# Moving the streamed and loaded operands of a matmul to other distances in SBUF, stage by stage

## The chip, the cores and the metric

One core of a Trainium2 chip runs the whole program. The metric is the device time of one execution in microseconds (us). The kernel before takes 986.3 us, the median of three runs (985.2 to 988.33).

## The reference

256 tokens of width 1024 go through one attention and feed-forward layer and then through two recurrent layers, all in float32.

```python
def reference(x, ...):
    x = first_block(x, mem, positions, ...)
    return second_block(x, c_2, ...)

def _layer(x, mem, positions, ...):
    h = _rms_norm(x, g_pre_mix)
    proj = h @ w_in                                   # 1024 x 8864
    y_mla, y_dil, y_mem = ...                         # three attention branches
    merged = gates0 * (y_mla @ w_br_mla) + gates1 * (y_dil @ w_br_dil) + gates2 * (y_mem @ w_br_mem)
    x = x + _rms_norm(merged @ w_o, g_post_mix)
    h2 = _rms_norm(x, g_pre_ffn)
    return x + _rms_norm(_conv_ffn(h2, w_ffn_up, conv_w, conv_b, w_ffn_down), g_post_ffn)

def second_block(x, c, ...):
    for l in range(2):
        h = rms_norm(x, norm_g[l]) * (1 + scale) + shift
        rg_x, rg_z, ml_x, ml_o, ml_z = split(h @ w_in[l])      # five products of 1024 x 1024
        y_rg = rglru(conv(rg_x)) * silu(rg_z)
        y_ml = mlstm_branch(ml_x, ml_o) * silu(ml_z)
        x = x + gate * (concatenate([y_rg, y_ml]) @ w_out[l])
    return rms_norm(x, final_g)
```

## The kernel before, in words

Nearly all of TensorE's time goes to products of activations with weights, and each is made of three matmuls. `load` (line 246) brings a block of weights of 128x1024 float32 from memory into a `raw` tile, ScalarE rounds it into `hi` (line 254) and VectorE takes the rest into `lo` (line 257). The activations are kept as two tiles in the same way, `H` and `L`. `prod` (line 261) then adds hi x H, hi x L and lo x H into PSUM. A matmul of TensorE has two operands: `lhsT` is loaded into the array (a weight load, PEld in the profile), `rhs` is streamed through it (PE). The weight load of a matmul runs while the matmul before it streams.

There are two roles:

- In `proj` (line 269) the weights are loaded, 128 columns at a time, and the activations are streamed, 256 columns at a time. In the profile these are `mm<-H,hi`, `mm<-L,hi` and `mm<-H,lo`; 48 of them make one projection of 256 output columns, and the page puts 16 of each kind to it. This is the H role.
- In `proj_long` (line 286) the activations are loaded, 128 tokens at a time, and the weights are streamed, 256 columns at a time. These are `mm<-hi,s` and `mm<-lo,s`, the output products: `w_o`, `w_down`, `w_out0` and `w_out1`. This is the O role. The values of the dilated attention (`w_dv`) use the same function with `H` and `L` as the loaded operand (`mm<-hi,H`).

There are four stages that fill `H` and `L` anew and then use them: the attention mix (29 projections, 33 to 335 us), the feed-forward's `w_up` (22, 358 to 481 us), layer 0 (20, 558 to 723 us) and layer 1 (20, 772 to 935 us). Each ends in its output product: `w_o`, `w_down`, `w_out0`, `w_out1`.

Where the operands lie is set by the pools. The rings for `hi` and `lo` start at 224 bytes modulo 256, and every 128-column or 256-column piece of them too. `H` and `L` (line 351) start at 160 modulo 256. The large slots of `sp` hold the loaded operands of the output products (`gH`, `gL`, `aH`, `aL`, `yrH`, `yrL`, `ymH`, `ymL`) at 32 modulo 256, and with `stream=True` other operands at 160. So the distance, the streamed address minus the address that is being loaded for the next matmul, modulo 256, is 192 in both roles: 160 - 224 and 224 - 32. The exceptions are the dilated values at 224 - 160 = 64, and single pairs of 0, 64 and 128 where one kind of matmul follows another, as where `of_head` (line 967) puts two matmuls of `selR` between two projections.

The scheduler of the Tile layer orders the instructions.

Of the kernel before, what the change touches and what calls it, by code (L numbers as in the profile page):

```python
# [10 lines left out]
F32 = mybir.dt.float32  # L11
F32R = mybir.dt.float32r
# [6 lines left out]
P = 128  # L19
S = 256  # L20
D = 1024
KT = D // P
# [5 lines left out]
RAW, HI, LO = 4, 4, 4  # L28
FENCE = 4
STREAM = 32  # L30
HOLD = 3
MIX = """gc0 lr ms0 gc1 ln ms1 mt0 gc2 my0 ms2 mt1 lq0 my1 lq1 ms3 mt2 lq2 my2 lq3 mt3 lk my3 lv gc3
    ls0 bc0 bc1 ls1 bc2 bc3 lt0 dp0 ly0 ls2 lt1 x1 dp1 ly1 ls3 lt2 x1 dp2 ly2 ls4 lt3 x1 dp3 ly3 ls5 lt4 x1 dp4 ly4 ls6 lt5 x1 dp5 ly5 ls7 lt6 x1 dp7 ly6 lt7 x1 ga0 ly7 x1 dp6 x1
# [164 lines left out]
def block_kernel(ctx: ExitStack, tc: tile.TileContext, T: dict, out: bass.AP):  # L198
# [3 lines left out]
    cp = ctx.enter_context(tc.tile_pool(name="cp", bufs=1))  # L202
# [3 lines left out]
    fill = ctx.enter_context(tc.tile_pool(name="fill", bufs=1))  # L206


    dve.memset(fill.tile([P, 16], F32, name="fill"), 0.0)
    sp = ctx.enter_context(tc.tile_pool(name="sp", bufs=1))  # L210
    fill2 = ctx.enter_context(tc.tile_pool(name="fill2", bufs=1))
# [9 lines left out]
    def sm_tile():  # L221
        return smp.tile([P, 512], F32, name="sm", tag="sm")

    def slot(i, dt=F32, stream=False):
        a = STREAM if stream else 0
        return sp.tile([P, KT * S + 64], dt, name=f"s{i}", tag=f"s{i}")[:, a:a + KT * S].rearrange("p (k n) -> p k n", k=KT)

    def two():
        return t2.tile([P, 2, S], F32, name="two", tag="two", bufs=3)

    def one():
        return t2.tile([P, S], F32, name="one", tag="one", bufs=6)
# [48 lines left out]
    def urgent(on=True):  # L281

        return tc.high_priority(offset=URGENT) if on else nullcontext()
# [37 lines left out]
    def kth(t):  # L321
        return lambda k: t[:, k]
# [6 lines left out]
    def col(name, i=0, n=1):  # L329
        return cols[:, COL[name] + i:COL[name] + i + n]  # L330

    memT = slot(7)
    xn = cp.tile([P, 2, D], F32, name="xn")
    ones_s = cp.tile([P, S], F32, name="ones_s")
# [13 lines left out]
    half = cp.tile([P, 56], F32, name="half")  # L348

    dve.memset(cp.tile([P, STREAM], F32, name="fill3"), 0.0)  # L350
    HT = [cp.tile([P, KT, S], F32R, name=n) for n in ("H", "L")]
    dve.memset(cp.tile([P, STREAM], F32, name="fill4"), 0.0)
    H, L = kth(HT[0]), kth(HT[1])
    HT2, LT2 = HT


    def square(src):
# [104 lines left out]
    def rows_of(i):  # L462
        return slot(i).rearrange("p (t a) n -> p t (a n)", t=2)

    def spread(r):

        ps = sm_tile()[:, :S]
        for t in range(2):
            pe.matmul(ps[:, t * P:(t + 1) * P], lhsT=r[:, t:t + 1].to_broadcast([P, P]), rhs=ident, start=True, stop=True)
        return ps  # L470

    def kept(ps):
        r = t2.tile([P, S], F32, name="rstd", tag="rstd", bufs=3)
        act.copy(r, ps)
        return r
# [9 lines left out]
    def split_scaled(hi, lo, src, scale):  # L485
        return (act.activation(hi, src, AF.Identity, scale=scale),
                dve.scalar_tensor_tensor(out=lo, in0=src, scalar=scale, in1=hi.bitcast(F32), op0=ALU.mult, op1=ALU.subtract))

    def split(hi, lo, src, scale=None):
        if scale is None:  # L490
            act.copy(hi, src)  # L491
            dve.tensor_tensor(out=lo, in0=src, in1=hi.bitcast(F32), op=ALU.subtract)
        else:
            act.mul(hi, src, scale)  # L494
            dve.scalar_tensor_tensor(out=lo, in0=src, scalar=scale, in1=hi.bitcast(F32), op0=ALU.mult, op1=ALU.subtract)
# [21 lines left out]
    def ada_steps(n):  # L517

        for _ in range(n):
            if n_ada[0] < 50:  # L520
                next(ada[n_ada[0] // 25])
            n_ada[0] += 1


    with tc.tile_pool(name="l1", bufs=1) as l1, tc.tile_pool(name="pS", bufs=1) as pS:
        dve.memset(l1.tile([P, STREAM], F32, name="fill5"), 0.0)
        mask = l1.tile([P, S], F32, name="mask")
# [2 lines left out]
        ada += [ada_blocks(0, c_act), ada_blocks(1, c_act)]  # L530


        mH, mL = slot(0, F32R, True), slot(1, F32R, True)
        dma.dma_start(out=memT[:, 0:2], in_=T["memT"][:, 0:2])
        kv = [load(T["w_memkv"][0])]
        dma.dma_start(out=memT[:, 2:4], in_=T["memT"][:, 2:4])
# [55 lines left out]
        for quarter in (0.0, 0.25):  # L592
# [10 lines left out]
            t = l1.tile([P, S], F32, name=f"trig{len(trig)}")  # L603
# [5 lines left out]
        dve.tensor_scalar(out=half[:, 0:24], in0=col("b_gate", 0, 24), scalar1=0.5, scalar2=None, op0=ALU.mult)  # L609
        dve.tensor_scalar(out=half[:, 24:56], in0=col("rg_b_a_2", 0, 32), scalar1=0.5, scalar2=None, op0=ALU.mult)  # L610

        cH, cL = slot(4, F32R, True), slot(5, F32R, True)
        c_sq = []
        kpe = scratch[:, 5]
        for j in range(3):
            ps = proj("w_c", j, KT, H, L)
            for m in range(2):
                i = 2 * j + m
# [6 lines left out]
                else:  # L625
                    t = one()
# [193 lines left out]
        for step in MIX.split():  # L820
            n, i = step.rstrip("0123456789"), int(step.lstrip("abcdefghijklmnopqrstuvwxyz_") or 0)
# [26 lines left out]
            elif n == "dp":  # L848
                p = i // 8
# [18 lines left out]
                ada_steps(i)  # L868


        gH, gL = slot(4, F32R), slot(5, F32R)
        for j in range(4):
            jj = slice(2 * j, 2 * j + 2)
            split(gH[:, jj], gL[:, jj], merged[:, jj], 0.5)
# [3 lines left out]
    def row(i, t=None):  # L878
        if t is None:
            t = rows.tile([P, D], F32, name="row", tag="row")  # L880
        pool.dma_start(out=t, in_=T["rows"][i:i + 1, :].broadcast_to([P, D]))
        return t

    def post_norm(name, kt, Hf, Lf, hold, g, sums, nxt, beside):
        z = rows_of(6)
        n = len(LONG) - 1
        acc = small.tile([P, 2, n + 1], F32, name="accn", tag="accn", bufs=2)
        for j in range(n + 1):
            jj = slice(LONG_AT[j], LONG_AT[j + 1])
            ps = proj_long(name, kt, j, Hf, Lf, hold, beside[j])  # L890
            if j == n:
                pre = [load(T[nxt][b]) for b in range(2)]
            else:
                for t in range(2):
                    sq = square_sum(ps[t], acc[:, t, j:j + 1])
                    dve.tensor_tensor(out=z[:, t, jj], in0=ps[t], in1=g[:, jj], op=ALU.mult)
            if j == 0:
                root_table(sq)
        x_sum = small.tile([P, 2, 2], F32, name="xsum", tag="xsum", bufs=2)
        stat = [Rstd(acc[:, t]) for t in range(2)]  # L900
        fl = Flip()
        for t in range(2):
            with urgent():
                square_sum(ps[t], acc[:, t, n:n + 1])
                ins = dve.tensor_tensor(out=z[:, t, jj], in0=ps[t], in1=g[:, jj], op=ALU.mult)
                rz = stat[t].get()
                for i, (a, b) in enumerate(PARTS):
                    dve.scalar_tensor_tensor(out=xn[:, t, a:b], in0=z[:, t, a:b], scalar=rz, in1=xn[:, t, a:b], op0=ALU.mult, op1=ALU.add)
                    if sums:
                        square_sum(xn[:, t, a:b], x_sum[:, t, i:i + 1])  # L910
                r = Rstd(x_sum[:, t]).get() if sums else None
            fl.add(t, r)
        return x_sum, fl, pre, ins
# [3 lines left out]

    with urgent():  # L920
        for k in range(KT):
            last = split_scaled(HT2[:, k], LT2[:, k], fl(k), col("g_pre_ffn", k))
# [5 lines left out]
    for t in range(2):  # L928
        dve.tensor_copy(r[:, t:t + 1], Rstd(x_sum[:, t]).get())
    rs = kept(spread(r))  # L930
    aH = [slot(i, F32R) for i in (0, 1, 2)]
    aL = [slot(i, F32R) for i in (3, 4, 5)]
    with tc.tile_pool(name="fp", bufs=2) as fp:
        for f in range(FT):
            ps = proj("w_up", f, KT, H, L) if f else proj_first(pre, H, L)
# [13 lines left out]
            t = one()  # L949
            act.activation(t, z[:, 0], AF.Silu)  # L950
            dve.tensor_tensor(out=t, in0=t, in1=z[:, 1], op=ALU.mult)
            split(aH[f // 8][:, f % 8], aL[f // 8][:, f % 8], t)
    _, fl, pre, late = post_norm("w_down", FT, lambda k: aH[k // 8][:, k % 8], lambda k: aL[k // 8][:, k % 8], HOLD, row(1), True, "w_mlx0", ADA_DOWN)
    ada_steps(25 - n_ada[0])
# [54 lines left out]
                                         in1=dst[:, m, s:], op0=ALU.mult, op1=ALU.add)  # L1009

    for l in range(2):

        gcol = small.tile([P, 8], F32, name="gcol", tag="gcol", bufs=2)
        with tc.issue_after(late.ins):
# [18 lines left out]
            act.copy(gate[:, 512 * b:512 * b + 512], pgs[b])  # L1033


        xmH, xmL, xcH, xcL = (slot(i, F32R, i > 1) for i in range(4))
        vN, xr = slot(4), slot(5)
        xrH, xrL = slot(6, F32R, True), slot(7, F32R, True)
        gp = sm_tile()[:, :S]
        n_g = [0]  # L1040
        wm = {}
# [81 lines left out]
        for step in ORDER.split():  # L1123
            i = int(step[1])
# [50 lines left out]
        for j in range(4):  # L1175
            if j % 2 == 0:
                hi, lo = load(T[f"w_rg{l}"][j // 2])
            for h in (2 * j, 2 * j + 1):
# [4 lines left out]
                t = two()  # L1183
# [58 lines left out]
        def numerator(h):  # L1242
            pt = pts[h]
            nu = sm_tile().rearrange("p (a b) -> p a b", a=2)
            for m in range(2):
                es = slice(m * P, (m + 1) * P)
                pe.matmul(nu[:, m, 0:P], lhsT=vN[:, 2 * h, es], rhs=pt[:, 0:P], start=True, stop=True)
                pe.matmul(nu[:, m, P:S], lhsT=vN[:, 2 * h, es], rhs=pt[:, 2 * P:3 * P], start=True, stop=False)
                pe.matmul(nu[:, m, P:S], lhsT=vN[:, 2 * h + 1, es], rhs=pt[:, P:2 * P], start=False, stop=True)
            jj = slice(2 * h, 2 * h + 2)  # L1250
            dve.scalar_tensor_tensor(out=hn[:, jj], in0=to[:, jj], scalar=1.0, in1=nu, op0=ALU.add, op1=ALU.mult)
            return square(hn[:, jj])
# [8 lines left out]
            dve.tensor_tensor(out=t, in0=t, in1=src, op=ALU.mult)  # L1261
            split(dH, dL, t)

        yrH, yrL = slot(0, F32R), slot(1, F32R)
        sq = [numerator(0), numerator(1)]
        for j in range(4):
            jj = slice(2 * j, 2 * j + 2)
# [16 lines left out]
                    dp = in_parts("M", da)  # L1284
            if l == 0:
                ada_steps(ADA_RGZ[j])
        ymH, ymL = slot(2, F32R), slot(3, F32R)
        for j in range(4):
            jj = slice(2 * j, 2 * j + 2)
            ps = proj(f"w_mlz{l}", j, KT, H, L)  # L1290
# [8 lines left out]
        n = len(LONG) - 1  # L1299
# [56 lines left out]
```

## Time and profile before

| what | before |
|---|---|
| median of 3 runs | 986.3 us (985.2 to 988.33) |
| the profiled execution | 987.47 us, span 985.8 us |
| TensorE matmul busy | 953.3 us, 97% of the span |
| VectorE busy | 735.2 us, 75% |
| ScalarE busy | 626.7 us, 64% |
| mean granted TensorE clock | 0.995 of full speed |

The profiled execution is 1.2 us above the median of the runs, and 1.7 us of it lie around the span. Busy time of TensorE counts overlapped matmuls once: each lasts 276 ns or more from its start to its modelled end, but a new one starts every 113 to 118 ns.

### The profile page before, as it was taken

The page shows a single profiled execution, that of the slowest core. Times are in us where ns is not written, and L with a number is a line of the kernel's source. Part 1 is how long each engine was busy: PE and PEld are TensorE (multiplying, and loading weights), DVE is VectorE, ACT ScalarE, POOL GpSimd, SP SyncE. Part 2 cuts the span into 40 slices and gives each one's busy share as a digit, 9 for nine tenths or more (in the row PEclk, how much of TensorE's full clock was granted, in tenths as well). Part 3 has the DMA queues.
Part 4 walks back from the last instruction along what each step waited for, and adds up shares of the span by engine and source line. Part 5 has one row for each costly group of instructions (what it writes and reads, how often), then busy time and mean ns, then how long its engine had stood idle before and what let it go on. Part 6 is the DMA issues. An engine that isn't in the chain of part 4 may idle for free.

```text
span 985.8 us, 19651 instructions
## 1 busy us (share of the span) xinstructions
PE 953.3 (97%) x7880; PEld 916.2 (93%) x7880; DVE 735.2 (75%) x1281; ACT 626.7 (64%) x1042; POOL 53.8 (5%) x61
## 2 busy tenths in 40 slices
PE   7999999999999999999989999999999999999997
PEld 5999999899989989999989899898999998899997
DVE  5856766567565888888856788589986798687754
ACT  7666555454345578887744776895645677886643
POOL 0000000000000002111200000000001000000021
PEclk9999999999999999999999999999999999999999
DMA  8654576777786766565667365355786464345552
GB/s 300 212 177 129 176 230 209 249 235 225 250 252 205 224 194 205 183 197 186 204 219 240 126 210 163 120 170 162 250 268 219 131 209 152 108 128 193 172 177 80
DMA packets 53371, 190.74 MB, mean 193 GB/s; under 512 B 6080, under 2 KB 6464, under 8 KB 53280
## 3 DMA queue, kind: packets, MB, share of 16 engines
q1 hardware_dynamic: 52272, 185.17, 58.0%
q0 software_dynamic: 1008, 4.33, 1.4%
q8 instruction: 61, 1.00, 0.4%
q14 instruction: 30, 0.25, 0.1%
HBM read 188.42 MB, written 1.05 MB: 192 GB/s over the span
## 4 chain that ended last, share of the span: by engine, by line
PE 66%; DVE 12%; ACT 10%; DMA 7%; issue 4%; POOL 0%; DVEq 0%; SPq 0%; ACTq 0%; POOLq 0%
PE mm L266 56%; DVE lo L257 5%; DMA raw<-in_w_ada 5%; ACT hi L254 3%; ACT fz L945 2%; ACT fw L946 2%; DVE fu L939 1%; PE sm L1051 1%; ACT s L491 1%; DMA raw<-in_w_dv 1%; DVE raw L504 1%; PE sm L1256 1%; PE sm L1207 1%; PE sm L669 1%; DMA raw<-in_w_mlx 1%
## 5 line engine op out<-in xcount | busy, mean ns | idle before, releaser
L257 DVE TENSOR_TENSOR lo<-raw,hi 128x1024 fp32r<-128x1024 f32 (+2 forms) x300 | 369.6, 1244 | 95.6 <-ACT hi L254 93.8
L254 ACT CAST hi<-raw 128x1024 fp32r<-128x1024 f32 (+2 forms) x300 | 308.7, 1040 | 153.0 <-PE mm L266 80.1
L266 PE MATMUL mm<-H,hi 128*128 128x256 f32 x1456 | 236.9, 281 | 0.1
L266 PE MATMUL mm<-H,lo 128*128 128x256 f32 x1456 | 233.4, 278 | 1.4 <-DVE lo L257 1.4
L266 PE MATMUL mm<-L,hi 128*128 128x256 f32 x1456 | 234.2, 279 | 0.1
L266 PEld LDWEIGHTS mm<-H,hi 128*128 128x128 f32 x1456 | 197.6, 189 | 2.2 <-DVE s L1008 0.8
L266 PEld LDWEIGHTS mm<-H,lo 128*128 128x128 f32 x1456 | 197.6, 189 | 1.6 <-DVE lo L257 1.6
L266 PEld LDWEIGHTS mm<-L,hi 128*128 128x128 f32 x1456 | 197.7, 189 | 0.7 <-DVE L L1029 0.3
L266 PE MATMUL mm<-hi,s 128*128 128x256 f32 (+1 forms) x1032 | 148.0, 283 | 0.2 <-ACT s L494 0.2
L266 PEld LDWEIGHTS mm<-hi,s 128*128 128x128 f32 x1032 | 131.8, 189 | 1.9 <-ACT s L494 0.4
L504 DVE CUSTOM_DVE_ANT_0 raw<-raw,c_act 128x1024 f32<-128x1024 f32 x48 | 59.3, 1235 | 63.4 <-DMA raw<-in_w_ada 63.4
L266 PE MATMUL mm<-lo,s 128*128 128x256 f32 (+1 forms) x516 | 84.9, 284 | 5.7 <-DVE lo L257 5.7
L266 PEld LDWEIGHTS mm<-lo,s 128*128 128x128 f32 x516 | 70.5, 190 | 7.0 <-DVE lo L257 6.1
L266 PE MATMUL mm<-s,hi 128*128 128x256 f32 x320 | 53.5, 286 | 0.0
L266 PEld LDWEIGHTS mm<-s,hi 128*128 128x128 f32 x320 | 44.3, 190 | 6.3 <-PE mm L266 2.5
L438 ACT ACTIVATE sq<-xn 128x256 f32<-128x256 f32 (+1 forms) x28 | 14.3, 511 | 43.6 <-POOL xn L1320 32.6
L266 PE MATMUL mm<-s,lo 128*128 128x256 f32 x160 | 34.2, 281 | 0.0
L945 ACT ACTIVATE fz<-fu,cols 128x256 f32<-128x256 f32 x44 | 26.2, 595 | 7.6 <-DVE fu L939 7.6
L948 POOL TENSOR_TENSOR fz<-fz,fw 128x508 f32<-128x508 f32 x22 | 24.7, 1125 | 109.1 <-DVE fz L947 109.1
L491 ACT CAST s<-two 128x512 fp32r<-128x512 f32 x24 | 14.9, 619 | 22.7 <-DVE two L1261 22.7
L657 ACT ACTIVATE sx<-sx,nm 128x256 f32<-128x256 f32 (+3 forms) x24 | 13.3, 555 | 24.6 <-DVE nm L654 24.6
L266 PEld LDWEIGHTS mm<-s,lo 128*128 128x128 f32 x160 | 25.4, 189 | 2.0 <-issue 1.2
(320 smaller groups left out, 1152.1 us busy)
## 6 DMA issues: line engine op xcount, KB each, us to landing
raw<-in_w_ada SPq DMA_DIRECT2D x48, 512.0 KB, 4.5
raw<-in_w_up SPq DMA_DIRECT2D x44, 512.0 KB, 4.4
raw<-in_w_out SPq DMA_DIRECT2D x32, 512.0 KB, 4.3
raw<-in_w_down SPq DMA_DIRECT2D x20, 512.0 KB, 4.3
raw<-in_w_mlx SPq DMA_DIRECT2D x16, 512.0 KB, 4.3
raw<-in_w_rgx SPq DMA_DIRECT2D x16, 512.0 KB, 4.2
raw<-in_w_mlo SPq DMA_DIRECT2D x16, 512.0 KB, 3.8
raw<-in_w_rgz SPq DMA_DIRECT2D x16, 512.0 KB, 4.3
```

The costliest lines, as they stand in the source:

```text
L254: act.copy(hi[:, :n], raw)
L257: dve.tensor_tensor(out=lo[:, :n], in0=raw, in1=hi[:, :n].bitcast(F32), op=ALU.subtract)
L266: pe.matmul(dst, lhsT=t[x], rhs=t[y], start=(first and i == 0), stop=(last and i == n - 1))
L438: return act.activation(sq[:, :src.shape[-1]], src, AF.Square, accum_out=acc)
L491: act.copy(hi, src)
L504: dve.tensor_tensor_reduce(out=raw, in0=raw, in1=c_act, op0=ALU.mult, op1=ALU.add, scale=1.0, scalar=0.0, accum_out=mod[:, l, m:m + 1])
L657: act.activation(sx[:, a:b], src, AF.Exp, bias=nm[:, i:i + 1], accum_out=den[:, i:i + 1])
L669: pe.transpose(ps[:, i * P:(i + 1) * P], sx[:, o:o + P], ident)
L939: dve.tensor_tensor(out=u, in0=ps, in1=rs.unsqueeze(1).to_broadcast([P, 2, S]), op=ALU.mult)
L945: act.activation(z[:, i], u[:, i], AF.Identity, scale=col("conv_w", 88 + c), bias=col("conv_b", c))
L946: act.activation(w[:, i], u[:, i], AF.Identity, scale=col("conv_w", c))
L948: pool.tensor_tensor(out=z[:, :, 2:], in0=z[:, :, 2:], in1=w[:, :, :S - 2], op=ALU.add)
```

## The change

`H` and `L` get 64 more elements, and each of the four stages uses them at an offset of its own (`H_AT`, in elements of 4 bytes). The slots that hold the loaded operands of the four output products get an offset of their own too (`O_AT`). The distances modulo 256 become:

| stage | H role, before | H role, after | O role, before | O role, after |
|---|---|---|---|---|
| mix, then `w_o` | 192 | 80 | 192 | 176 |
| `w_up`, then `w_down` | 192 | 176 | 192 | 200 |
| layer 0, then `w_out0` | 192 | 184 | 192 | 80 |
| layer 1, then `w_out1` | 192 | 200 | 192 | 184 |

The dilated values go from 64 to 176. All other products keep 192. No instruction is added, taken away or moved: on every engine the two programs read the same, row for row, and only addresses differ. In absolute terms `H` and `L` start at 48, 144, 152 and 168 modulo 256 in place of 160, and the loaded operands of the output products at 48, 24, 144 and 40 in place of 32.

```diff
+H_AT = (36, 60, 62, 2)
+O_AT = (4, 62, 28, 2)
...
-    def slot(i, dt=F32, stream=False):
-        a = STREAM if stream else 0
+    def slot(i, dt=F32, a=0):
         return sp.tile([P, KT * S + 64], dt, name=f"s{i}", tag=f"s{i}")[:, a:a + KT * S].rearrange("p (k n) -> p k n", k=KT)
...
-    HT = [cp.tile([P, KT, S], F32R, name=n) for n in ("H", "L")]
+    HT = [cp.tile([P, KT * S + 64], F32R, name=n) for n in ("H", "L")]
+
+    def acts(stage):
+        return [t[:, H_AT[stage]:H_AT[stage] + KT * S].rearrange("p (k n) -> p k n", k=KT) for t in HT]
+
...
-    H, L = kth(HT[0]), kth(HT[1])
-    HT2, LT2 = HT
+    HT2, LT2 = acts(0)
+    H, L = kth(HT2), kth(LT2)
...
-        gH, gL = slot(4, F32R), slot(5, F32R)
+        gH, gL = slot(4, F32R, O_AT[0]), slot(5, F32R, O_AT[0])
...
+    HT2, LT2 = acts(1)
+    H, L = kth(HT2), kth(LT2)
...
-    aH = [slot(i, F32R) for i in (0, 1, 2)]
-    aL = [slot(i, F32R) for i in (3, 4, 5)]
+    aH = [slot(i, F32R, O_AT[1]) for i in (0, 1, 2)]
+    aL = [slot(i, F32R, O_AT[1]) for i in (3, 4, 5)]
...
     for l in range(2):
+        HT2, LT2 = acts(2 + l)
+        H, L = kth(HT2), kth(LT2)
...
-        yrH, yrL = slot(0, F32R), slot(1, F32R)
+        yrH, yrL = slot(0, F32R, O_AT[2 + l]), slot(1, F32R, O_AT[2 + l])
...
-        ymH, ymL = slot(2, F32R), slot(3, F32R)
+        ymH, ymL = slot(2, F32R, O_AT[2 + l]), slot(3, F32R, O_AT[2 + l])
```

## Rows read from the trace of the kernel before

**Rows 1.** Page, part 1: busy time, share of the span, instructions.
```profile
PE 953.3 (97%) x7880; PEld 916.2 (93%) x7880; DVE 735.2 (75%) x1281; ACT 626.7 (64%) x1042; POOL 53.8 (5%) x61
```

**Rows 2.** Chain of waits: 48 matmuls of one product: start us, us, what.
```profile
163.49 5.46 PE mm L266 x48
171.08 5.65 PE mm L266 x48
...
891.47 5.66 PE mm L266 x48
899.64 5.46 PE mm L266 x48
```

**Rows 3.** Windows, matmuls of line 266: stretch, us, busy (count), PEclk, DMA share, GB/s.
```profile
39.00:70.00 31.00, 31.00 (x266) 1.00 0.64 203
365.00:479.00 114.00, 114.00 (x1008) 1.00 0.61 195
510.00:534.00 24.00, 24.00 (x206) 1.00 0.69 230
724.00:766.00 42.00, 42.00 (x373) 1.00 0.75 237
937.00:977.00 40.00, 40.00 (x355) 1.00 0.38 130
```

**Rows 4.** Timeline of TensorE, 716.0 to 717.9: start us, us, instruction and count.
```profile
716.27 0.62 PE L266 MATMUL mm<-L,hi 128*128 128x256 f32 x4
716.72 0.62 PE L266 MATMUL mm<-H,lo 128*128 128x256 f32 x4
717.18 0.28 PE L971 MATMUL sm<-Mh,selR 128*128 128x256 f32 x1
717.29 0.28 PE L971 MATMUL sm<-Ml,selR 128*128 128x256 f32 x1
717.41 0.63 PE L266 MATMUL mm<-H,hi 128*128 128x256 f32 x4
717.88 0.28 PE L266 MATMUL mm<-L,hi 128*128 128x256 f32 x1
```

**Rows 5.** Timeline of TensorE, 922.6 to 924.3.
```profile
922.39 0.63 PE L266 MATMUL mm<-L,hi 128*128 128x256 f32 x4
922.86 0.64 PE L266 MATMUL mm<-H,lo 128*128 128x256 f32 x4
923.33 0.27 PE L971 MATMUL sm<-Mh,selR 128*128 128x256 f32 x1
923.44 0.28 PE L971 MATMUL sm<-Ml,selR 128*128 128x256 f32 x1
923.56 0.62 PE L266 MATMUL mm<-H,hi 128*128 128x256 f32 x4
924.01 0.50 PE L266 MATMUL mm<-L,hi 128*128 128x256 f32 x3
```

**Rows 6.** Windows, as rows 3: the slow stretches of the mix's H role (8).
```profile
37.10:70.90 33.80, 33.80 (x289) 1.00 0.64 206
...
307.90:313.50 5.60, 5.60 (x47) 1.00 0.67 233
sum 78.80, PE 78.75; mean PE 9.84
```

**Rows 7.** Windows, as rows 3: the other slow stretches (17) whose distance changes.
```profile
170.80:176.50 5.70, 5.66 (x48) 1.00 0.82 268
282.40:288.00 5.60, 5.60 (x47) 1.00 0.90 266
333.40:335.50 2.10, 2.10 (x19) 1.00 0.81 189
480.70:490.70 10.00, 10.00 (x87) 1.00 0.66 209
...
929.20:934.90 5.70, 5.66 (x48) 1.00 0.56 185
sum 157.60, PE 157.27; mean PE 9.25
```

**Rows 8.** ScalarE and VectorE writing H and L: ns min/median/max, first and last.
```profile
L487 DVE SCALAR_TENSOR_TENSOR L<-sm,cols,H x16: 475/478/484, 31.0 to 362.3; 128x256 fp32r<-128x256 f32 x16
L1027 ACT ACTIVATE H<-sm,mod x8: 557/581/603, 557.2 to 774.8; 128x256 fp32r<-128x256 f32 x8
```

More of the change, by code (lines that the diff above doesn't have):

```diff
@@ L530, in block_kernel @@
         ada += [ada_blocks(0, c_act), ada_blocks(1, c_act)]
-        mH, mL = slot(0, F32R, True), slot(1, F32R, True)
+        mH, mL = slot(0, F32R, STREAM), slot(1, F32R, STREAM)
         dma.dma_start(out=memT[:, 0:2], in_=T["memT"][:, 0:2])
@@ L610, in block_kernel @@
         dve.tensor_scalar(out=half[:, 24:56], in0=col("rg_b_a_2", 0, 32), scalar1=0.5, scalar2=None, op0=ALU.mult)
-        cH, cL = slot(4, F32R, True), slot(5, F32R, True)
+        cH, cL = slot(4, F32R, STREAM), slot(5, F32R, STREAM)
         c_sq = []
@@ L1033, in block_kernel @@
             act.copy(gate[:, 512 * b:512 * b + 512], pgs[b])
-        xmH, xmL, xcH, xcL = (slot(i, F32R, i > 1) for i in range(4))
+        xmH, xmL, xcH, xcL = (slot(i, F32R, STREAM * (i > 1)) for i in range(4))
         vN, xr = slot(4), slot(5)
-        xrH, xrL = slot(6, F32R, True), slot(7, F32R, True)
+        xrH, xrL = slot(6, F32R, STREAM), slot(7, F32R, STREAM)
         gp = sm_tile()[:, :S]
```

## The prediction

> **What bounds the kernel now.** I read the engines' busy times first. TensorE is busy for 97% of the span and no other engine for more than 75% [rows 1], so the time is the time between the starts of its matmuls, and the change touches nothing else. The second view is the chain of waits, where the projections show up as pieces of 48 matmuls: two neighbours of the same size take 5.46 and 5.65 us, and in layer 1 it is 5.66 and then 5.46 [rows 2]. The third view, windows that count matmuls, says what that is. From 365 to 479 us 1,008 matmuls overlap 114.0 us, from 724 to 766 us 373 overlap 42.0 us; a matmul lasts about 276 ns, so some two of each count hang over the edges: 114.0 / 1,006 and 42.0 / 371 are both 113.3 ns from start to start. From 510 to 534 us it is 24.0 / 204 = 117.6 ns and from 39 to 70 us 31.0 / 264 = 117.4 ns [rows 3]. There are two periods, the fast of 113.3 ns and the slow of about 117.8 (33.8 us for 287 in the longest stretch [rows 6]; the chain's pieces differ by 0.19 to 0.20 us over 48, some 4.1 ns; I take 117.8 - 113.3, in round 4.45 ns). The granted clock is 1.00 of full speed, the 2.4 GHz level, in both.
>
> A stretch keeps its period until something disturbs it. The timeline shows what does. At 717 us four matmuls take 0.45 us (716.27 to 716.72), then two matmuls of another operand pass, and afterwards four take 0.47 us (717.41 to 717.88) [rows 4]. At 923 us it goes the other way: 0.47 us before, 0.45 after [rows 5]. At just these places the distance is 128 for one or two pairs. So the period depends on where streaming and loading stand to each other, and distance can switch it, both ways.
>
> **The change part by part.** No instruction is added, removed or moved; what changes is the distance under some 5,950 matmuls: 4,368 in the H role (91 projections of 48), 1,488 in the O role (192 + 528 + 384 + 384) and the 96 dilated values that stream 256 columns. Its cost is the number of matmuls that change period times 4.45 ns, and each counts in full, since TensorE's pieces are on the chain in every stage.
>
> What could be won: the slow stretches whose distance changes are 78.8 us in the mix's H role [rows 6] and 157.6 us elsewhere [rows 7]. At the fast period they would take 4.45 / 117.8 = 3.8% less: 3.0 + 6.0 = 9.0 us. That is the bound below, unless a period under 113.3 ns exists, which no row shows. What could be lost: all 5,950 slow cost 26.5 us, of which 9.0 are paid already: 17.5 us more. That is the bound above, as long as 117.8 ns is the worst period; a pair at distance 0 or 64 is at most a few ns longer where it stands alone.
>
> Between the two ends I go by the nearest distances the trace has.
>
> - 176, 184 and 200 are within 16 bytes of 192. At 192 the longest stretches are fast throughout (`w_up`, both `w_out` [rows 3]), so a fast period at these distances is the nearer end. I take it that the slow stretches there (157.6 us: values, `w_o`, `w_down`, both layers' H role [rows 7]) go: -6.0 us.
> - 80 is 16 bytes from 64, and the two stretches at 64, the dilated values, are both slow (the first two of [rows 7]). In the mix 78.8 us of about 29 x 48 x 115.5 ns = 161 us are slow now, half; I take three quarters: 0.25 x 1,392 x 4.45 ns = +1.5 us. `w_out0`, all fast now, I take at half slow: 0.5 x 384 x 4.45 ns = +0.9 us.
> - The writes of `H` and `L` by ScalarE and VectorE start at other addresses. They take 478 to 581 ns each [rows 8], eight of each open a stage, and those are waited for. Between no effect and a tenth more, 4 x 8 x 0.05 = 1.6 us; I take 0, since no row shows one that depends on its address.
>
> The sum is -6.0 + 1.5 + 0.9 = -3.6 us. Against the profiled execution, 987.47 us, that is 983.9 us; that execution was 1.2 us above the median of its runs, so I predict **982.7 us** as the median. A measurement of this kernel can tell about 0.3%, 3.0 us, from no change: faster means under 983.3 us, slower over 989.3 us.
>
> The Trainium skill ("SBUF — State Buffer", section "SBUF: two separate sides") says that TensorE never waits on anyone for its SBUF port and that the port for weight loads is an independent second one. By that the distance could not matter and the change would be worth 0. Rows 3 to 5 speak against it: same shape, same clock, two periods, switched by a pair at another distance. I go by the rows; the rule's outcome is the first rival.
>
> **The rivals.**
>
> First, the period is chosen where a stretch starts, not by the distance. For it: of two projections of equal form some are slow and some fast at the same 192 (rows 2 have both in layer 1), and many stretches begin after matmuls of other kinds. Then the changed distances draw anew, with a similar share, and the time stays within 2 us or so: 986.3 us. Against it: the two stretches at 64 are both slow, and the switches at 128.
>
> Second, and slower: starts that are only 8 bytes aligned disturb the fast period. 184 and 200 put `H` and `L` of layers 0 and 1 at 152 and 168, and the loaded operands of `w_down` and `w_out1` at 24 and 40; every f32r operand of the kernel before starts at 32 modulo 64, so no row shows such a start. The 2,832 matmuls (960 + 960 + 528 + 384) would then all run at 117.8 ns. Of them 157.6 - 13.4 = 144.2 us, 1,224 matmuls, are slow already ([rows 7] without its first three); 1,608 x 4.45 ns = +7.2 us and the rest as before: 993.5 us. It decides if more than some 670 matmuls (3.0 us / 4.45 ns) beyond today's turn slow on balance. If the 16-byte shifts do it too, the end is the bound above, 1,003.8 us. For it: the fast period at 192 is kept over 1,000 matmuls, so it has most to lose. The Trainium skill ("SBUF — State Buffer", section "Specifications (TRN2)") gives lines of 16 bytes in SBUF and a penalty for each crossing into a new one, which by 8-byte starts would be one more per row; no run here shows its price.
>
> Third, every slow stretch goes, at 80 too: -9.0 us, 977.3 us. For it: nothing in the rows but that 80 was never tried.
>
> **How the numbers follow.** The forecast has 0.36, the first rival 0.27, the second 0.31 with its extreme, the third 0.06. Forecast and third are faster: 0.42. The first is no change: 0.27. The second is slower: 0.31. Both signs are well in it, since a distance near a good one is the only evidence for the gain. The range must reach from the third rival's time to beyond the second's: 977 to 997 us leaves out a little of the gain and the extreme loss, some 12%. The forecast's own range is 980 to 984 us.
>
> **What would show it.** In the changed profile, 48 matmuls on the chain should take 5.46 us in layers 0 and 1 and not 5.65, and the window of `w_down` should count 113.3 ns from start to start. In the mix more projections should take 5.65 than now. The forecast is wrong if `w_up` (176) or `w_out1` (184) show 117 ns and more, if a third period turns up, or if the shares of slow stretches stay as they are. If the writes of `H` take over 0.6 us, the third bullet was wrong.

## The result, and the profile after

The kernel with the new distances takes 1004.06 us, the median of 4 runs (1003.38 to 1004.88), against 986.91 us for the kernel before (median of 4, 985.2 to 988.33): a ratio of 1.0175 with an interval of 1.0156 to 1.0194. It is slower by 17 us, where I had predicted 982.7 us and a range that ended at 997. The profiled execution has a span of 1002.3 us, 16.5 us more than before, at a granted clock of 0.999.

The page of the kernel after, part 1, answers to [rows 1].

```profile
PE 976.2 (97%) x7880; PEld 940.6 (94%) x7880; DVE 727.9 (73%) x1281; ACT 630.6 (63%) x1042; POOL 52.7 (5%) x61
```

The instructions are as many as before. VectorE and ScalarE are busy as long as before, within 1%. TensorE's busy time has grown by 22.9 us, from 953.3 to 976.2, and that of its weight loads by 24.4; no other engine's grew by more than 3.9. The same matmuls start further apart.

Where they do is seen in windows that begin and end at the same matmuls in both kernels. First the kernel before, matmuls of line 266: stretch, us, busy (count), PEclk, DMA share, GB/s.

```profile
39.00:70.80 31.80, 31.80 (x273) 1.00 0.64 203
339.60:353.20 13.60, 13.60 (x123) 1.00 0.84 276
366.70:477.80 111.10, 111.10 (x983) 1.00 0.61 197
559.40:580.00 20.60, 20.60 (x178) 1.00 0.50 160
726.70:767.60 40.90, 40.28 (x356) 1.00 0.75 238
773.50:793.40 19.90, 19.90 (x178) 1.00 0.50 161
939.70:975.90 36.20, 36.20 (x322) 1.00 0.37 125
```

Then the kernel after, where the same line is 269. The rows are, in this order, the mix (now at 80), `w_o` (176), `w_up` (176), layer 0 (184), `w_out0` (80), layer 1 (200) and `w_out1` (184).

```profile
40.20:72.60 32.40, 32.40 (x273) 1.00 0.65 200
343.50:357.70 14.20, 14.20 (x122) 1.00 0.81 270
370.70:487.50 116.80, 116.80 (x982) 1.00 0.60 191
566.10:587.10 21.00, 21.00 (x177) 1.00 0.55 165
735.80:778.30 42.50, 41.99 (x356) 1.00 0.70 225
784.30:805.40 21.10, 21.10 (x177) 1.00 0.53 169
954.50:992.30 37.80, 37.80 (x322) 1.00 0.35 116
```

Every row is longer, at the same clock. As in the prediction, a part of each count hangs over the edges, here 2.4 (276 / 113.3), so `w_up` went from 111.1 / 980.6 = 113.3 ns from start to start to 116.8 / 979.6 = 119.2 ns. The mix runs at 119.7 ns, `w_o` at 118.7, layer 0 at 120.3, layer 1 at 120.9 and `w_out1` at 118.3. None of these is 113.3, and all are above the 117.8 ns that I had taken for the worst. A count is a whole number: one matmul more or less moves the period of a window of 177 by 0.7 ns and that of `w_o`'s window by 1 ns, so only `w_up` and the output products of the layers tell it to 0.4 ns or better.

The starts of the rows say what each stage added to the time. The kernel after is late by 1.2 us at 39 us, by 3.9 at `w_o`, 4.0 at `w_up`, 6.7 at layer 0, 9.1 at `w_out0`, 10.8 at layer 1, 14.8 at `w_out1` and 16.4 at its end. The end of `w_up` is late by 9.7 us, so `w_up` lost 5.7, and between it and layer 0 3.0 us came back. There `w_down` runs, and TensorE waits there for `lo`. Its waits in that stage, before (480.7 to 556 us) and after (490.6 to 563 us): engine and line, what it waited for, us in total, times, longest.

```profile
PE mm L266 <- DVE lo L257: 5.7, 2, 4.5
```

```profile
PE mm L269 <- DVE lo L260: 2.9, 3, 1.6
```

The waits fell by 2.8 us: TensorE comes later to the weights of `w_down` and waits less for them. Over the whole span its idle time fell by 22.9 - 16.5 = 6.4 us, and so much of what the matmuls lost was given back. Waits for `lo` are 4.6 us of that (8.6 before, 4.0 after).

The chain of the kernel after answers to [rows 2]: start us, us, what.

```profile
122.43 5.46 PE mm L269 x48
128.22 5.69 PE mm L269 x48
...
212.54 5.76 PE mm L269 x48
```

```profile
806.83 5.46 PE sm L269 x48
...
943.85 5.82 PE mm L269 x48
```

The two pieces of 5.46 us are products that the change leaves at 192. Every other whole piece of 48 that the chain shows in the mix and the layers takes 5.68 to 5.82 us; before, 5.46 and 5.65 stood side by side. The mix has two lengths at its one distance of 80, 5.68 to 5.69 and 5.75 to 5.76 us: more than one period is not a matter of 192 alone.

The writes of `H` and `L`, by line, answer to [rows 8]; the three numbers are the shortest, the median and the longest in ns.

```profile
L494 DVE SCALAR_TENSOR_TENSOR L<-sm,cols,H x16: 473/475/484, 32.2 to 366.9; 128x256 fp32r<-128x256 f32 x16
L1038 ACT ACTIVATE H<-sm,mod x8: 557/578/598, 563.9 to 785.5; 128x256 fp32r<-128x256 f32 x8
```

They take 475 and 578 ns, and took 478 and 581.

### The profile page after: what moved, and what is told of

Read it like the earlier page. It is cut to its first block, busy times and chain, and to the rows that moved or that the text cites. A ratio compares the mean times of both kernels' runs of the same rounds, so it can differ in the third digit from the quotient of the medians.

```text
span 1002.3 us, 19651 instructions
## 1 busy us (share of the span) xinstructions
PE 976.2 (97%) x7880; PEld 940.6 (94%) x7880; DVE 727.9 (73%) x1281; ACT 630.6 (63%) x1042; POOL 52.7 (5%) x61
## 4 chain that ended last, share of the span: by engine, by line
PE 78%; DVE 8%; DMA 8%; ACT 2%; issue 2%; POOL 0%; DVEq 0%; SPq 0%; ACTq 0%; POOLq 0%
PE mm L269 67%; DMA raw<-in_w_ada 5%; DVE lo L260 3%; DMA raw<-in_w_down 2%; PE sm L269 1%; PE sm L1062 1%; DMA raw<-in_w_dv 1%; DVE raw L511 1%; ACT hi L257 1%; PE sm L1218 1%; PE sm L1267 1%; PE sm L676 1%; PE sm L737 0%; PE sm L463 0%; DVE two L822 0%
## 5 line engine op out<-in xcount | busy, mean ns | idle before, releaser
L260 DVE TENSOR_TENSOR lo<-raw,hi 128x1024 fp32r<-128x1024 f32 (+2 forms) x300 | 361.8, 1217 | 118.1 <-ACT hi L257 116.8
L269 PE MATMUL mm<-H,hi 128*128 128x256 f32 x1456 | 243.3, 285 | 0.1
L269 PE MATMUL mm<-L,hi 128*128 128x256 f32 x1456 | 240.4, 283 | 0.4 <-DVE L L494 0.2
L269 PE MATMUL mm<-H,lo 128*128 128x256 f32 x1456 | 239.5, 283 | 0.2 <-DVE lo L260 0.2
L269 PEld LDWEIGHTS mm<-H,hi 128*128 128x128 f32 x1456 | 202.1, 190 | 2.2 <-issue 1.2
L269 PEld LDWEIGHTS mm<-L,hi 128*128 128x128 f32 x1456 | 203.1, 190 | 1.1 <-DVE L L494 0.7
L269 PEld LDWEIGHTS mm<-H,lo 128*128 128x128 f32 x1456 | 202.6, 190 | 0.4 <-DVE lo L260 0.4
L269 PE MATMUL mm<-hi,s 128*128 128x256 f32 (+1 forms) x1032 | 150.7, 286 | 0.2 <-ACT s L501 0.2
L269 PE MATMUL mm<-y,hi 128*128 128x256 f32 x192 | 26.0, 278 | 0.0
```

The source lines that it names most:

```text
L260: dve.tensor_tensor(out=lo[:, :n], in0=raw, in1=hi[:, :n].bitcast(F32), op=ALU.subtract)
L269: pe.matmul(dst, lhsT=t[x], rhs=t[y], start=(first and i == 0), stop=(last and i == n - 1))
```

## The experiments

The theory that the traces suggest: 113.3 ns is held at distance 192 and hardly anywhere else, so nearness to 192 is worth nothing. Its rivals: it is the 8-byte starts (the prediction's second rival), or multiples of 32 or 64 would have done, or one role alone carries the loss. In what follows "start" is an operand's address modulo 64; in the kernel before it is 32 for every f32r operand, that is, for every `hi`, `lo`, `H`, `L` and the other tiles that these products load or stream. Each run is compared with the kernel before on the same chip, whose median was between 983.67 and 986.95 us.

### 8-byte starts at an unchanged distance

All f32r operands of the kernel before are moved by 8 bytes (start 40), so that every distance stays. The room comes from fill tiles that go, from a ring of three `rstd` tiles that becomes two and one of two `diag` tiles that becomes one.

```diff
-        a = STREAM if stream else 0
+        a = (STREAM if stream else 0) + (18 if dt == F32R else 16)
...
-        hi = hip.tile([P, 1024], F32R, name="hi", tag="hi")
+        hi = hip.tile([P, 1088], F32R, name="hi", tag="hi")[:, 2:2+1024]
...
```

> Every streamed and loaded f32r operand of the kernel before is moved by 8 bytes, so all start at 40 modulo 64 in place of 32, and every distance stays as it was (192, and 64 for the dilated values). To make room two small scratch rings are one buffer shorter. Theory A (what counts is the distance: a stretch can only hold 113.3 ns when streamed and loaded rows lie alike within 64 bytes): w_up and both w_out at 113.3 ns, the time 985 to 989 us. Theory B (what counts is the start address itself, an 8-byte start costs a line more per row): w_up and w_out at 117 ns and more, the time 1,000 us or more.

Measured: 1017.22 us against 986.95, ratio 1.0319 (1.0245 to 1.0393). Windows of this kernel, `w_up` and `w_out1`, columns as above:

```profile
376.50:495.60 119.10, 119.10 (x982) 1.00 0.60 188
...
965.90:1004.80 38.90, 38.90 (x322) 1.00 0.35 112
```

These are 119.1 / 979.6 = 121.6 ns and 38.9 / 319.6 = 121.7 ns. So a start that is only 8-byte aligned loses the fast period by itself, at 192 too, and costs more than the slow period of before. The shorter rings are not the cause: a kernel below has the same rings at another start and runs at 113.3 ns. But the mix and `w_up` of the change start on 16 bytes and are slow as well; this is not the whole cause.

### Other distances without 8-byte starts

Two kernels have the code of the change with other offsets; `hi` and `lo` stay where they were. One has distances that are multiples of 64, at starts as before: H role 128, 64, 0, 192 and O role 0, 128, 64, 128, in the order of the stages.

```diff
-H_AT = (36, 60, 62, 2)
-O_AT = (4, 62, 28, 2)
+H_AT = (48, 32, 16, 0)
+O_AT = (48, 16, 32, 16)
```

> The changed kernel with distances that are multiples of 64: H role 128, 64, 0, 192, O role 0, 128, 64, 128. Theory A: each of these can hold 113.3 ns as 192 does, some stretches slow, some fast in every stage, the time 982 to 996 us. Theory C (192 alone is good, each other distance meets loading and streaming in the same place): w_up at 64, w_out0 at 64, w_out1 at 128 all at 117.5 ns or more, the time about 1,000 us.

Measured: 996.6 us in a single run, against 986.95. Windows of this kernel: mix (128), `w_up` (64), layer 0 (0), layer 1 (192).

```profile
39.70:72.10 32.40, 32.40 (x273) 1.00 0.62 199
...
369.20:484.60 115.40, 115.40 (x982) 1.00 0.61 194
562.30:583.30 21.00, 21.00 (x177) 1.00 0.56 182
...
780.40:800.30 19.90, 19.90 (x178) 1.00 0.53 162
```

The window of layer 1, the one that kept 192, is at 19.9 / 175.6 = 113.3 ns in a kernel in which the windows of all the others are at 117.8 (64) to 120.3 (0). That is the theory in one view.

The other has the odd multiples of 32: H role 160, 224, 96, 32 and O role 32, 160, 224, 96. The operands that move start at 0, the weights still at 32.

```diff
-H_AT = (36, 60, 62, 2)
-O_AT = (4, 62, 28, 2)
+H_AT = (56, 8, 40, 24)
+O_AT = (40, 8, 56, 24)
```

> The changed kernel with distances that are odd multiples of 32: H role 160, 224, 96, 32, O role 32, 160, 224, 96. All starts are multiples of 32 bytes. Theory A: no stretch holds 113.3 ns, all run at 117 to 121 ns, the time 1,000 to 1,006 us. Theory B: the starts are as even as before, so the fast period is there as before and the time 984 to 990 us.

Measured: 1000.44 us in a single run, against 986.95. Windows of this kernel, `w_up` (224) and layer 1 (32):

```profile
370.20:486.20 116.00, 116.00 (x982) 1.00 0.61 192
...
783.40:804.00 20.60, 20.60 (x177) 1.00 0.53 164
```

118.4 and 118.0 ns, and the other stages lie at 117.9 to 119.8. Both sides of 192, 160 and 224, are no better than 32. A price that rises steadily with the distance from 192 doesn't show.

### One role at a time

The change in the output products alone: `H_AT = (0, 0, 0, 0)`.

> Only the O role's part of the change (176, 200, 80, 184); the H role and the dilated values as before. Both A and B: the output products stay at 117.5 to 118.7 ns, which costs 0.9 us in w_o, 0.9 in w_down, 1.8 in w_out0 and 1.9 in w_out1 over before, 5.5 us in all: about 992 us. Less than 3 us over before would mean that other work hides it.

Measured: 990.24 us against 986.95, ratio 1.0028 (1.0006 to 1.005), so +3.3 us. Windows of this kernel, `w_up` (192 again) and `w_out1` (184):

```profile
368.40:479.40 111.00, 111.00 (x982) 1.00 0.62 196
...
940.90:978.80 37.90, 37.90 (x323) 1.00 0.36 119
```

`w_up` is back at 113.3 ns, `w_out1` stays slow at 118.2, though the stage ahead of it is at 192 again. I had expected 5.5 us, and TensorE's busy time did grow by 5.8, from 953.3 to 959.1; the time grew by less, as with the whole change.

The change in the H role alone: `O_AT = (0, 0, 0, 0)`, so that all output products have 192 again.

> Only the H role's part of the change (80, 176, 184, 200, with the dilated values at 176); the output products back at 192. If the two parts add up: 1,004.1 - 3.3 (what e4 cost) = 1,000.8 us, with layer 0 at 120.3 ns and layer 1 at 121 ns as in the changed kernel and both w_out at 113.3 ns. If the H role's cost is hidden by other work, clearly less, under 997 us.

Measured: 1000.64 us against 983.67, ratio 1.0192 (1.0163 to 1.0222): as much as the whole change. Windows of this kernel, mix (80), `w_up` (176), `w_out0` and `w_out1` (both 192):

```profile
40.10:72.00 31.90, 31.90 (x272) 1.00 0.61 199
...
369.70:486.60 116.90, 116.90 (x982) 1.00 0.56 191
...
733.60:774.50 40.90, 40.30 (x356) 1.00 0.69 231
...
950.60:988.30 37.70, 37.70 (x323) 1.00 0.34 115
```

`w_out0` takes its 40.9 us of before, but `w_out1`, at 192 and fast before, is at 37.7 / 320.6 = 117.6 ns, and `w_o` at 117.9. The two parts, 3.3 and 17.0, are more than the 17.2 of the whole, but their intervals are too wide to say that they don't add. The time is what I expected, 1,000.8 us, the periods are not: at 192 a stretch can go either way, and here two of the three output products named, each after a slow stage, came out slow. So nearly all of the change's loss is there with the H role alone, and giving `w_o` and `w_out1` their 192 back saved little in this run.

The mix is a surprise: 31.9 / 269.6 = 118.3 ns, where the change has 119.7 in the same stretch, with the same instructions and the same addresses of both operands. A distance away from 192 has no single price either, and a difference of some 1.5 ns between two stretches needn't come from their distances.

### Which starts matter

Two kernels keep all distances at 192 and move the start: by 16 bytes, in the way of the first experiment (start 48), and by 32, with a fill tile of eight more elements (start 0).

```diff
+        a = (STREAM if stream else 0) + (20 if dt == F32R else 16)
...
+        hi = hip.tile([P, 1088], F32R, name="hi", tag="hi")[:, 4:4+1024]
...
```

> As e1, with 16 bytes: every streamed and loaded f32r operand starts at 48 modulo 64, every distance as in the kernel before (192). Theory D (distance 192 and starts at whole multiples of 32 bytes are both needed): no stretch at 113.3 ns, w_up at 118 to 121 ns, the time 1,000 to 1,012 us, below e1's 1,017. Theory E (only starts inside a 16-byte line hurt): w_up and both w_out at 113.3 ns again, the time 985 to 992 us.

```diff
-    dve.memset(cp.tile([P, STREAM], F32, name="fill3"), 0.0)
+    dve.memset(cp.tile([P, STREAM + 8], F32, name="fill3"), 0.0)
```

> The kernel before with a filler of 32 bytes more, so that every streamed and loaded f32r operand starts at a whole multiple of 64 and every distance stays 192. Theory D: both periods as before, w_up and w_out at 113.3 ns, the time 984 to 990 us. If it was the place 32 within 64 bytes that mattered, w_up runs at 117 ns and more and the time is 1,000 us or more. A period below 113.3 ns would be new.

Measured with start 48: 983.79 us in a single run, against 983.67. Its page, part 1, and its windows of the mix, `w_up` and layer 0:

```profile
PE 947.5 (96%) x7880; PEld 911.5 (93%) x7880; DVE 735.3 (75%) x1279; ACT 626.5 (64%) x1042; POOL 54.0 (5%) x61
```

```profile
40.00:70.60 30.60, 30.60 (x272) 1.00 0.64 210
...
365.40:476.50 111.10, 111.10 (x983) 1.00 0.56 195
558.90:578.70 19.80, 19.80 (x177) 1.00 0.55 185
```

The mix, 117.4 ns before, is at 30.6 / 269.6 = 113.5, and layer 0 at 113.4: the slow period of the kernel before is gone from these stretches, and 5.8 us of TensorE's busy time with it. The theory by which a 16-byte shift hurts as an 8-byte one does fell. The time didn't follow, as far as one run can tell: the kernel before ran from 981.28 to 986.54 us on this chip. I put it down to the single `diag` tile and the two `rstd` tiles, but no run shows that; what the trace shows is that the waits for `lo` are 10.7 us, against 8.6 in the kernel before.

Measured with start 0: 982.45 us against 983.67, ratio 0.9992 (0.9973 to 1.0011), no change. Its chain has both periods, as the kernel before has:

```profile
596.74 5.65 PE mm L266 x48
646.64 5.47 PE mm L266 x48
```

So at 192 there are three cases: starts at 0 or 32 have both periods, at 48 only the fast, at 40 only a third of 121.6 ns. The dilated values stay at 64 in all of these, and at start 48 their two pieces of 48 take 5.47 and 5.65 us: there 64 has both.

The next kernel keeps start 48 and both `diag` tiles; `rstd` is again a ring of two. The room comes from a constant tile of 1/32 that is dropped; its factor moves into the copy ahead of it.

```diff
+EDGE = 4
...
-        a = STREAM if stream else 0
+        a = (STREAM if stream else 0) + 16 + (EDGE if dt == F32R else 0)
...
-                act.copy(part, self.part)
+                act.mul(part, self.part, 1.0 / 32.0)
...
```

> e5 without its cost in scratch rings: every streamed and loaded f32r operand starts at 48 modulo 64, every distance of the kernel before is kept, one ring is a buffer shorter and one constant tile is gone. Theory F (16-byte odd starts at 192 leave only the fast period): 113.4 to 114 ns in all stages, some 8 us less of TensorE's time than in the kernel before; if all of it reached the end 978 us against 986, but e5 kept only a part of it on the path, so 980 to 984 us, and at least 2 us under the kernel before on the same chip. Theory D (multiples of 32 are needed) has fallen with e5 and would have given 1,000 us.

Measured: 983.42 us (12 runs) against 985.39 (17 runs), ratio 0.997 (0.9954 to 0.9986). Its page, part 1, its chain in layer 1, and its largest wait on TensorE:

```profile
PE 947.1 (96%) x7880; PEld 910.7 (93%) x7880; DVE 734.8 (75%) x1278; ACT 626.4 (64%) x1042; POOL 53.3 (5%) x61
```

```profile
889.19 5.48 PE mm L263 x48
897.18 5.47 PE mm L263 x48
```

```profile
PE mm L263 <- DVE lo L254: 10.3, 6, 3.9
```

It beats the kernel before by 2.0 us, 0.3%, and the change by far more. In the profiled executions TensorE is busy 6.2 us less than before, where I had expected some 8, but the span is only 3.2 us shorter (982.6 against 985.8): the waits for `lo` rose from 8.6 to 10.3 us, so part of the gain became a wait for weights, the reverse of what the change did in `w_down`.

### Does the better start save other distances?

Start 48, with distances 128, 64, 0, 32 in the H role and 0, 128, 64, 96 in the O role (and a single `diag` tile). In layer 1 and `w_out1` the operand that moves starts at 16.

> e2's test at e5's starts: all operands at 48 modulo 64, H role 128, 64, 0, 32 and O role 0, 128, 64, 96 (the last of each with one operand at 16). Theory F1 (with these starts any distance is good): 113.3 to 114 ns throughout, the time 980 to 986 us. Theory F2 (the distance has to be 192 at any start): 117 ns and more in w_up, w_out0 and w_out1, the time 995 us or more.

Measured: 1000.86 us in a single run, against 985.39. Windows of this kernel, mix (128), `w_up` (64), layer 0 (0) and `w_out1` (96):

```profile
39.00:71.40 32.40, 32.40 (x272) 1.00 0.64 201
...
371.00:482.10 111.10, 111.10 (x983) 1.00 0.61 198
564.20:584.90 20.70, 20.70 (x177) 1.00 0.55 178
...
950.70:989.10 38.40, 38.40 (x322) 1.00 0.36 117
```

The start doesn't save them: 118.6 to 120.2 ns. The exception is `w_up`, which holds 113.3 ns at 64, so neither theory holds throughout. With start 32 it had 117.8 there, and `w_out0`, at 64 and start 48 in this kernel, has 118.0. This is the one place away from 192 at which a long stretch was fast.

### 8 bytes in the streamed or in the loaded operand

The code of the change with distances 104, 40, 208 and 144 in both roles. The first two of each role put the operand that moves on 8 bytes, the others on 16.

```diff
-H_AT = (36, 60, 62, 2)
-O_AT = (4, 62, 28, 2)
+H_AT = (42, 26, 4, 52)
+O_AT = (22, 38, 60, 12)
```

> Four distances not tried yet, in both roles: mix and w_o 104, w_up and w_down 40, layer 0 and w_out0 208, layer 1 and w_out1 144. Streamed rows start at 8 bytes into a 16-byte unit in the mix and w_up, at whole units in both layers; loaded ones likewise in w_o and w_down, and in w_out0 and w_out1. Theory G (off 192 every distance costs 4 to 6 ns, and a streamed row that starts 8 bytes into 16 costs 1 to 3 ns more): mix and w_up at 120 to 122 ns, layers 0 and 1 at 117.5 to 119.5 ns, all four output products at 117.5 to 120 ns, the time 1,002 to 1,006 us. Theory H (each distance has a price of its own and starts do not matter): H and O role alike at the same distance, within 0.7 ns.

Measured: 1003.19 us in a single run, against 984.72. Windows of this kernel, mix (104), `w_o` (104), `w_up` (40), a stretch of `w_down` (40), layer 0 (208) and `w_out1` (144):

```profile
39.20:71.70 32.50, 32.50 (x273) 1.00 0.64 200
343.70:357.70 14.00, 14.00 (x122) 1.00 0.82 263
371.20:488.80 117.60, 117.60 (x982) 1.00 0.59 189
493.00:511.00 18.00, 18.00 (x152) 1.00 0.67 221
568.10:588.90 20.80, 20.80 (x177) 1.00 0.59 181
...
953.10:991.50 38.40, 38.40 (x323) 1.00 0.36 117
```

Where the streamed rows start on 8 bytes it is 120.1 ns, in the mix and in `w_up` alike; where they start on 16, 119.1 in layer 0. Where the loaded operand starts on 8 bytes it is 14.0 / 119.6 = 117.1 ns in `w_o`, but 18.0 / 149.6 = 120.3 in `w_down`, no less than `w_up` at the same 40. And `w_out1`, with no operand on 8 bytes, is at 38.4 / 320.6 = 119.8. So this run doesn't show in which role the 8 bytes cost, nor that they cost anything on top of a distance that is slow already: the differences are of about the size that two runs of the mix at 80 have between them. The theory of the same price in both roles fell at 104, where the roles are 3 ns apart. The other had `w_o` at 117.5 or more; its window gives 117.1, which a count can't tell from that.

One more rival can be settled from the windows above: that the place of the streamed operand alone decides, and not its distance. In layer 0 `H` starts at 176 modulo 256 here (160 + 16), and it does so in the first kernel with start 48, at distance 192. There the stretch runs at 113.4 ns, here at 119.1; what differs is where the loaded weights lie, at 240 there and at 224 here.

## Why the prediction was wrong

**What bounds the kernel** was right in the main. TensorE's periods decide, the clock is not in it, and distance switches the period. That there are two periods held for the kernel before; the change brought others, up to 120.9 ns.

**The first bullet failed.** "176, 184 and 200 are within 16 bytes of 192 … so a fast period at these distances is the nearer end" took the price for one that changes slowly with the distance. It doesn't: in their windows 160, 176, 184, 200, 208 and 224 all run at 117 to 121 ns, and near 192 nothing else is fast. The forecast of -6.0 us for the stretches there has to be replaced by what they did: `w_up`, put at 0, cost +5.7 us in its window alone, and `w_out1` +1.6; by the starts of the rows layers 0 and 1 lost 2.4 and 4.0 us where they were to gain.

**The second bullet** had the sign and about half the size. At 80 three quarters of the mix were to be slow and half of `w_out0`, +1.5 and +0.9 us. In the mix every piece at 80 on the chain is slow, and slower than the old slow period (119.7 ns in the window); the starts of the rows give the stage 2.7 us. `w_out0` is busy 41.99 - 40.28 = 1.7 us longer: all of it is slow, by 4 to 5 ns a matmul.

**The third bullet** held: the writes of `H` and `L` are unchanged, 0 us.

**The bound above** was 1,003.8 us, and the median is 1004.06. That they agree is partly chance. The bound had all 5,950 matmuls at 117.8 ns, +17.5 us; they run at 118 to 121, and TensorE's busy time grew by 22.9 us. What brought it near was a term that the sum didn't have: 6.4 us of idle time that a slower TensorE no longer had. The step "each counts in full, since TensorE's pieces are on the chain in every stage" was therefore wrong too, in `w_down` above all, and the kernel that beats both shows it from the other side, where 6.2 us less of matmuls gave 3.2 us of span. The chain of the kernel before could have told: inside the mix it leaves TensorE at 219 us for VectorE and for loads, and comes back to it only at 299 us.

```profile
219.15 0.69 DVE two L815
...
299.69 5.46 PE mm L266 x48
```

**The rivals.** The first, the period drawn anew at each start of a stretch, would have left the time where it was, and fell as an account of the change. What it rests on is real: the run with the H role alone has `w_out1` slow at 192 where `w_out0` is fast. The second gave the end that came, in its extreme; its mechanism is half of the truth. Starts on 8 bytes cost, at 192 from 113.3 to 121.6 ns with both operands moved, but the stages of the change on 16 bytes lost as well, `w_up` at 176 the most. The wider loss is the distance's. The third rival fell.

The extreme was priced and named, but I gave it little and let the range stop at 997. The rows spoke for more: 192, the only distance with long fast stretches, was the only one for which a fast period was shown at all, and the other distances in [rows 4, 5] sat just where the period flipped.

The Trainium skill ("SBUF — State Buffer", section "SBUF: two separate sides") has TensorE never wait for its port, with a second one for weight loads. By that all these kernels would take the same time; they range from 113.3 to 121.7 ns a matmul, at one shape and one clock, so the measurement decides against it. The 16-byte lines of the Trainium skill ("SBUF — State Buffer", section "Specifications (TRN2)") agree in kind with starts at 40 and 48: 121.6 and 113.3 ns.

What stays open: by what mechanism the two addresses meet, and what picks one of the periods that a distance has. No run shows it. That 256 is the right modulus wasn't tested. Steps finer than 8 bytes weren't tried, and only 0, 32, 64, 96 and 128 were tried with the weights at two places, of which 64 alone gave both a fast and a slow stretch. Each kernel was profiled in one execution.

## What to carry to other kernels

Back-to-back matmuls of the same shape can have several periods, and here the addresses of the streamed and the loaded operand decided which were to be had: read the period from windows that count matmuls, and hold a distance that is shown to be fast rather than one near it. Try first the start of all operands together, which here (from 32 to 48 modulo 64, at an unchanged distance) took the slow period away and gave 2.0 us of 985. A gain or a loss per matmul reaches the end only as far as weights are ready: put a wait for weights beside each sum of this kind.

## What was not expected of the hardware

- A distance 8 to 32 bytes from the fast one is as slow as any other: of the 15 other than 192 that the windows show, 14 run at 117 to 121 ns in all of them; only 64 held 113.3, at start 48, in `w_up` and in one of the two pieces of the dilated values.
- At distance 192 the start of the operands alone makes three cases: both periods at 0 and 32 modulo 64, the fast alone at 48, and 121.6 ns at 40.
- The same stretch at the same addresses, the mix at 80, ran at 119.7 ns in one kernel and at 118.3 in another that differs only in the loaded operands of the output products, which come later.
